# Conformer-and-RWKV-7 block on one core: TensorE's order in phase 1 written by the kernel instead of by the scheduler

## The chip, the cores and the metric

The kernel runs on one core of a Trainium2 chip. The core has TensorE (PE in the profile, with its weight loads as PEld), VectorE (DVE), ScalarE (ACT), GpSimd (POOL) and SyncE, whose queue (SPq) issues nearly all transfers. The metric is device time in microseconds (us) of one launch, lower is better. A difference under 0.5% (15 us here) can't be told from no change.

## The reference

```python
mod = silu(c) @ ada_w + ada_b                      # shift, scale, gate
h = rmsnorm(x, norm_g) * (1 + scale) + shift       # x: 2048 tokens x 1024
p = h @ w_in                                       # one projection for both branches
# branch A: u = val * sigmoid(gate); causal depthwise conv of width 31; layernorm; swish; * silu(c_og); @ w_conv_out
# branch B: token shift of r, k, v, w_low, a_low; decay and a from two low-rank products; then per token and head
state = state * w_t - (state @ kk_t) b_t^T + v_t k_t^T     # 16 heads, state 64 x 64
o_t   = state @ r_t
# layernorm of o per head, + sum(r*k*r_k)*v, * silu(r_og), @ w_rwkv_out
m = sigmoid(g_conv) * y_conv + sigmoid(g_rwkv) * y_rwkv
out = rmsnorm(x + gate * (m @ w_out), final_g)
```

All of it is float32.

## The kernel before

The 2048 tokens are taken in four blocks of 512 (`TB`), the channels in tiles of 128. A float32 projection is done as three products of a rounded high part and a low part (`hi*hi`, `lo*hi`, `hi*lo`, line 210, `mm3k`): eight steps of 128 input channels, three products each, and each product cut into two of 256 columns, so that one projection tile is 48 matmuls on line 217. Weights come as float32 in block 0, are split by ScalarE (line 194) and GpSimd or VectorE (line 196), and are written back to memory; later blocks read the two halves. Seven buffers hold them.

**Phase 1** goes through the four blocks. A block begins with eight loads of the normed input and their split into `h_hi` and `h_lo` (`hprep`, line 376) and the low-rank tile (`lora_split`). Then come four groups of four heads, two pairs of heads each. For a group these small products are needed beside its projections:

- `pair` (line 476), once for each of the two pairs: the low-rank products (489 to 495), then from k the sums of squares (528), from r and k the products inside chunks of 64 tokens (558, two batches), from v its transposes (581) and the head sums (297, 298), and the transposes of the keys (599, two batches). They go through three accumulator buffers, `aux`.
- the first products with v (628), whose result is copied into `XO`;
- the inverse of the triangular 64 x 64 matrices: eight small tiles of 16 KB a pair are sent to memory, laid out anew, solved by GpSimd in 31 steps of two operations (656, 658), sent back, transposed by VectorE (684), and two batches of 32 x 32 products on TensorE merge them (688, 697);
- the **chain** over the eight chunks: c1 (715, state times k and r) -> VectorE adds (717) -> c2 (720, inverse times that) -> VectorE scales into `uv` (722) -> c3 (726, keys times uv) -> VectorE updates the state `S` (730) -> next chunk. These are 24 TensorE steps a group, each waiting for VectorE, and each chain waits for the one before;
- the outputs (739), added on VectorE into the even half of `XO` (744), normed there by VectorE, ScalarE and GpSimd (756 to 765), transposed on TensorE (770) and written out. `XO` has one buffer, so the next group's `XO` is set to zero (617) after that.

The other projections (convolution values and gates, output gates) need nothing of this: they fill. Each convolution tile costs VectorE 31 operations over 512 columns (802, 805). `xnorm` (341) norms the next block's tokens and transposes them on TensorE (359). In block 3 its place is taken by the first layer norm (`lnorm_first`) and the first gated outputs (`z_first`). Side work that prepares the weights of phase 2 (`keep`, `ogate`) stands in blocks 1 and 2. **Phase 2** does the three output projections and the final norm.

What sets the order: the program is written group by group, and a list scheduler with a simulated timeline (`schedule_with_timeline_sim=True`) chooses, on each engine, the next instruction by what it believes ready and by program order, raised by `high_priority`. On the chip each engine then takes its instructions in that fixed order, and an instruction that waits holds up all behind it.

## Time and profile before

| what | us |
|---|---|
| median of 3 runs (2982.64 to 2993.91) | 2986.47 |
| the profiled execution, its span | 2988.9 |
| phase 1, to the last product with h | about 2390 |
| phase 2 | about 599 |
| TensorE busy in the span | 2817.8 |
| VectorE, ScalarE, GpSimd busy | 2053.9, 941.8, 1251.6 |

The profiled execution's own time is its span, 2.4 us over the median. In a row of groups the columns are line, engine, operation, result<-operands, shape, count, busy us, mean ns of one, idle us before it and what ended that. A row of waits has who waited, for whom, us in all, times, longest. A row of stages has length, then busy time and count for each engine, then the granted TensorE clock as a share. A float32 product of TensorE appears in the trace as two instructions, in the order below as one.

### The profile page before, as it was taken

The numbers are of one execution on the slowest core, as the hardware profiler recorded it, in microseconds if no ns is written. First come the engines' busy times: TensorE is split into PE (matmuls) and PEld (weight loads), VectorE is DVE, ScalarE is ACT, GpSimd is POOL, SyncE is SP. The second block draws the span as 40 slices with busy tenths as digits, with TensorE's granted clock in tenths as the row PEclk, the third lists the DMA queues.
The fourth block names the chain that finished last, engine by engine and source line by source line (L and its number), as shares of the span: only waits on it lengthen the run. The fifth ranks groups of instructions, "written<-read, shape, count | busy, mean of one in ns | idle before, by whom it ended". The sixth has DMA issues, their size and how long they took to land.

```text
span 2988.9 us, 64784 instructions
## 1 busy us (share of the span) xinstructions
PE 2817.8 (94%) x25672; PEld 2647.3 (89%) x25672; DVE 2053.9 (69%) x3871; ACT 941.8 (32%) x1779; POOL 1251.6 (42%) x1786
## 2 busy tenths in 40 slices
PE   6889898999999999899999999999999999899998
PEld 6889898989899998899989988999989978688988
DVE  6677878787677676867776667777689535777433
ACT  5433434342324142324132414132333112333201
POOL 3556455534343435243434445526367104555000
PEclk9999999999999999999999999999999999999999
DMA  8666758664758589647565767656547678889774
GB/s 313 216 229 217 254 212 281 239 225 158 259 189 288 158 267 300 220 150 245 160 229 169 254 227 260 200 181 204 175 159 263 219 273 304 326 300 341 243 284 167
DMA packets 367697, 699.24 MB, mean 234 GB/s; under 512 B 135265, under 2 KB 154017, under 8 KB 367394
## 3 DMA queue, kind: packets, MB, share of 16 engines
q1 hardware_dynamic: 367394, 695.10, 68.5%
q8 instruction: 202, 3.31, 0.4%
q14 instruction: 101, 0.83, 0.1%
HBM read 506.14 MB, written 187.70 MB: 232 GB/s over the span
## 4 chain that ended last, share of the span: by engine, by line
PE 42%; DMA 16%; POOL 10%; DVE 10%; SPq 4%; issue 4%; ACT 2%; POOLq 0%; DVEq 0%; ACTq 0%
PE ps_main L217 31%; POOL TT L658 4%; POOL itmp L656 3%; DMA La<-dA 2%; DMA w_st<-w_in_t 2%; DVE acc L805 2%; PE pout L1126 1%; PE pout L1127 1%; PE pout L1128 1%; DMA w_gr<-grow_d 1%; DMA dT<-TT 1%; DMA xt<-x_in 1%; DMA w_st<-w_ro_t 1%; SPq L669 1%; PE xo L720 1%
## 5 line engine op out<-in xcount | busy, mean ns | idle before, releaser
L217 PE MATMUL ps_main<-h_hi,w_lo 128*128 128x256 f32 x4608 | 952.4, 285 | 18.2 <-POOL w_lo L196 9.8
L217 PE MATMUL ps_main<-h_hi,w_hi 128*128 128x256 f32 x4608 | 952.0, 285 | 17.0 <-ACT w_hi L194 6.0
L217 PE MATMUL ps_main<-h_lo,w_hi 128*128 128x256 f32 x4608 | 951.1, 285 | 0.0
L217 PEld LDWEIGHTS ps_main<-h_hi,w_hi 128*128 128x128 f32 x4608 | 720.4, 192 | 28.7 <-ACT w_hi L194 10.5
L217 PEld LDWEIGHTS ps_main<-h_hi,w_lo 128*128 128x128 f32 x4608 | 719.1, 192 | 28.1 <-POOL w_lo L196 11.5
L217 PEld LDWEIGHTS ps_main<-h_lo,w_hi 128*128 128x128 f32 x4608 | 719.0, 191 | 7.2 <-issue 0.5
L805 DVE SCALAR_TENSOR_TENSOR acc<-u,ck,acc 128x512 f32<-128x512 f32 x928 | 697.4, 752 | 19.9
L656 POOL TENSOR_TENSOR itmp<-La,TT 128x126 f32<-128x126 f32 (+22 forms) x496 | 180.3, 363 | 161.5 <-DMA La<-dA 126.4
L658 POOL TENSOR_TENSOR TT<-TT,itmp 128x126 f32<-128x126 f32 (+22 forms) x496 | 190.2, 383 | 36.8
L712 ACT ACTIVATE Se<-S,pe 128x128 f32<-128x128 f32 x256 | 88.8, 394 | 252.6 <-DVE S L730 252.3
L196 POOL TENSOR_TENSOR w_lo<-w_st,w_hi 128x1024 fp32r<-128x1024 f32 x47 | 115.0, 2447 | 126.7 <-ACT w_hi L194 115.1
L730 DVE TENSOR_TENSOR S<-xo,Se 64x128 f32<-64x128 f32 x256 | 73.4, 287 | 104.0 <-PE xo L726 99.8
L194 ACT CAST w_hi<-w_st 128x1024 fp32r<-128x1024 f32 x71 | 74.5, 1049 | 177.8 <-DMA w_st<-w_in_t 137.0
L722 DVE TENSOR_TENSOR uv<-xo,rn 64x256 f32<-64x256 f32 x128 | 53.8, 420 | 97.1 <-PE xo L720 95.7
L593 POOL TENSOR_TENSOR BK<-BK,pe 128x1024 f32<-128x1024 f32 x32 | 62.3, 1946 | 111.2 <-PE aux L558 83.5
L717 DVE TENSOR_TENSOR XO<-xo,XO 128x256 f32<-128x256 f32 x128 | 53.6, 418 | 78.4 <-PE xo L715 63.5
L715 PE MATMUL xo<-S,KR 128*128 128x128 f32 x512 | 82.7, 284 | 18.6 <-DVE S L730 18.5
L568 DVE TENSOR_TENSOR As<-aux,maskA 128x512 f32<-128x512 f32 x128 | 82.9, 684 | 21.0 <-PE aux L558 20.2
L817 ACT ACTIVATE th<-ps_main 128x512 f32<-128x512 f32 x64 | 38.2, 597 | 187.2 <-PE ps_main L217 175.3
L720 PE MATMUL xo<-XO,As 64*64 64x64 f32 x1024 | 90.2, 227 | 6.2 <-DVE XO L717 6.2
L720 PEld LDWEIGHTS xo<-XO,As 64*64 64x64 f32 x1024 | 70.7, 135 | 26.9 <-DVE XO L717 8.1
L558 PE MATMUL aux<-KR,BK 64*128 64x128 f32 x1024 | 91.7, 295 | 2.1 <-POOL KR L546 1.7
(303 smaller groups left out, 5292.6 us busy)
## 6 DMA issues: line engine op xcount, KB each, us to landing
w_hi<-kh_in SPq DMA_DIRECT2D x219, 512.0 KB, 5.3
w_lo<-kl_in SPq DMA_DIRECT2D x219, 512.0 KB, 4.1
w_st<-w_in_t SPq DMA_DIRECT2D x73, 512.0 KB, 4.7
kh_in<-w_hi SPq DMA_DIRECT2D x71, 512.0 KB, 2.9
kl_in<-w_lo SPq DMA_DIRECT2D x71, 512.0 KB, 3.6
w_hi<-kh_ro SPq DMA_DIRECT2D x32, 512.0 KB, 6.3
w_lo<-kl_ro SPq DMA_DIRECT2D x32, 512.0 KB, 5.5
w_hi<-kh_co SPq DMA_DIRECT2D x32, 512.0 KB, 4.7
```

Of the source, the lines that this page charges most:

```text
L194: nc.scalar.copy(hi, st)
L196: lo_eng.tensor_tensor(out=lo, in0=st, in1=hi.bitcast(F32), op=ALU.subtract)
L217: nc.tensor.matmul(ps[:, qs], ww[:, k, :], aa[k][:, qs], start=(k == 0 and t == 0 and q == 0), stop=(k == KT - 1 and t == 2 and q == ms - ...
L558: return nc.tensor.matmul(pA[hh][:, c // 2, es], BK[hs, cc, es], KR[hs, cc, es], start=(c == 0), stop=(c == 3), skip_group_check=True)
L568: nc.vector.tensor_tensor(out=Asb[:, hh, c4 * 4:c4 * 4 + 4, :].rearrange("p (a e) n -> p a (e n)", e=2), in0=pA[hh], in1=flat(maskA).unsqu ...
L656: nc.gpsimd.tensor_tensor(out=tmp[:, :ni, :nt], in0=La[:, j:j + 1, j + 1:].broadcast_to([P, ni, nt]), in1=TT[:, :ni, j:j + 1].broadcast_to ...
L658: nc.gpsimd.tensor_tensor(out=TT[:, :ni, j + 1:], in0=TT[:, :ni, j + 1:], in1=tmp[:, :ni, :nt], op=ALU.add)
L712: nc.scalar.mul(Se[:, q, :], Sg[:, q, :], R[q]["pe"][:, c:c + 1])
L715: nc.tensor.matmul(xo[:, q, :], R[q]["KR"][:, cc, es], Sg[:, q, :], start=(q == 0), stop=(q == 1), skip_group_check=True)
L720: nc.tensor.matmul(xo[pr_, q, hs], As[q][pr_, hh, c, kcol(e)], XO[pr_, c, q, hs], start=(q == 0 and hh == 0), stop=(q == 1 and hh == 1), s ...
L730: nc.vector.tensor_tensor(out=Sg[hs, :, hs], in0=xo[hs, 2:4, hs], in1=Se[hs, :, hs], op=ALU.add)
L805: nc.vector.scalar_tensor_tensor(out=acc if i + 1 < HALO else yj, in0=u[:, i:i + TB], scalar=ck[:, j, i:i + 1], in1=acc, op0=ALU.mult, op1 ...
```

## The change

TensorE's order in phase 1 is no longer chosen by the scheduler (`manual_schedule` for that engine alone; the other engines and the queues are ordered as before). The small products are written as generators, *threads*, that hand back a condition and a least gap in us. `compose` runs a clock that only adds the planned length of every product issued (`te`). It issues the first thread, by rank, whose condition holds and whose gap is over; else one step (six matmuls) of the next projection; and if there is none it moves the clock by 0.25.

```diff
+LSQ, LKR, LA2, LVV, LTK, LUV = 6.0, 6.0, 2.4, 4.0, 2.4, 1.5
+LCH, LINV, LNORM, LXN, LLOW = 3.0, 68.0, 30.0, 20.0, 8.0
+LOOK, DUO, LSIDE = 10, 2, 12.0
+    def te(us):
+        clock[0] += us
+        return nc.tensor
+    def compose(jobs):
+        while jobs or threads:
+            t_ = next((t_ for t_ in sorted(threads, key=lambda t_: t_.rank) if t_.ready()), None)
+            if t_ is not None:
+                t_.resume()
+                continue
+            j_ = pick(jobs)
+            if j_ is None:
+                clock[0] += 0.25
+                continue
...
+            if next(j_[1], None) is None:
+                jobs.remove(j_)
...
+            if c:
+                yield lch
             xo = px.tile([P, 4, P], F32, name="xo", tag="xo")
             for q in range(2):
-                nc.tensor.matmul(xo[:, q, :], R[q]["KR"][:, cc, es], Sg[:, q, :], start=(q == 0), stop=(q == 1),
-                                 skip_group_check=True)
+                te(0.22).matmul(xo[:, q, :], R[q]["KR"][:, cc, es], Sg[:, q, :], start=(q == 0), stop=(q == 1),
+                   skip_group_check=True)
             nc.vector.tensor_tensor(out=XO[:, c], in0=xo[:, 0:2], in1=XO[:, c], op=ALU.add)
+            yield lch
...
-        O = XO[:, 0::2]
+        done.add(("chain", G))
+        O = uv[:, 0:NCH // 2]
...
+        yield last(G, LNORM, 22.0)
         for q in range(2):
             pr = 2 * g + q
+            yield (late_free, 0.0)
...
+    def merge(G):
+        yield (lambda: G in inv, 0.0)
+        As, rn, uv, R = grp[G]
+        T11, at = inv.pop(G)
+        yield (lambda: clock[0] >= at + last(G, LINV, 60.0) and late_free(), 0.0)
```

In words, what else it does:

- Gaps: three us (`LCH`) after each chain step, 68 (`LINV`; 60 in the last group) from the second pair's products inside chunks to the merges, 30 (`LNORM`) from the outputs to their transposes, 20 (`LXN`) in `xnorm`, 6, 4 and 2.4 between steps of a pair (`LSQ`, `LKR`, `LVV`, `LTK`).
- The inverse is issued in the second pair's thread, right behind its products inside chunks, and no longer after the whole pair and the first products with v.
- The outputs go into the first half of `uv` (two buffers) instead of `XO`, and are normed there.
- The priorities of the work on the other engines: chain, merge and norm of outputs 8000 (`HPC`), `xnorm` 6000 (`HPX`), pairs 4000 (`HPP`). The tanh of gates and the low-rank split get 3000, as the weights' splits have.
- Loads of `xnorm`, `hprep`, `keep`, `ogate`, `z_first` and others get a dependency without a semaphore on the last TensorE instruction issued (`behind`), which places them in the scheduler's order. `keep` and `ogate` are a thread with 12 us between the halves.
- Two projections at a block's end and two at its beginning are interleaved step by step (`duo`), so that the inputs `h` are used up, and taken up, tile by tile.
- In block 3 the filling projections are spread over the groups in another way (`LP`).
- The number of operations on each engine is unchanged but for five instead of six weight splits a group on VectorE in block 0.

**Where chain and products inside chunks meet.** TensorE before, in the second group of block 1. L726 is c3, L715 the next chunk's c1, L558 the products inside chunks of a later pair, L217 a projection; S_422 is the second group's state.

```order
L726 MATMUL xo<-uv,tk 128x128 x2
L217 MATMUL ps_main<-h_lo,w_hi 128x256 x2
L217 MATMUL ps_main<-h_hi,w_lo 128x256 x2
L558 MATMUL aux<-KR,BK 128x128 x9
L217 MATMUL ps_main<-h_hi,w_hi 128x256 x2
L217 MATMUL ps_main<-h_lo,w_hi 128x256
L715 MATMUL xo<-S_422,KR 128x128 x2
```

The same meeting now, in the group after it (S_424); c3 is L843, c1 L830, the products inside chunks L652, a projection L303.

```order
L843 MATMUL xo<-uv,tk 128x128 x2
L652 MATMUL aux<-KR,BK 128x128 x8
L303 MATMUL ps_main<-h_hi,w_hi 128x256 x2
L303 MATMUL ps_main<-h_lo,w_hi 128x256 x2
L303 MATMUL ps_main<-h_hi,w_lo 128x256 x2
L303 MATMUL ps_main<-h_hi,w_hi 128x256 x2
L303 MATMUL ps_main<-h_lo,w_hi 128x256 x2
L303 MATMUL ps_main<-h_hi,w_lo 128x256 x2
L303 MATMUL ps_main<-h_hi,w_hi 128x256 x2
L303 MATMUL ps_main<-h_lo,w_hi 128x256 x2
L303 MATMUL ps_main<-h_hi,w_lo 128x256 x2
L830 MATMUL xo<-S_424,KR 128x128 x2
```

Between the two chain steps stood 7 projection matmuls, and now stand 18. Counted over all 383 distances between neighbouring chain steps, those with fewer than 12 projection matmuls between went from 64 to 7, those with 12 to 23 from 128 to 65, those with 24 to 29 from 146 to 99, and those with 30 to 36 from 27 to 197.

**Small products of a pair.** TensorE before, in block 1: v's transposes (L581) and, later, the head sums (L297, L298).

```order
L581 MATMUL aux<-ident,vv 128x128 x4
L217 MATMUL ps_main<-h_hi,w_hi 128x256 x2
L217 MATMUL ps_main<-h_lo,w_hi 128x256 x2
L217 MATMUL ps_main<-h_hi,w_lo 128x256 x2
L217 MATMUL ps_main<-h_hi,w_hi 128x256 x2
L217 MATMUL ps_main<-h_lo,w_hi 128x256 x2
L217 MATMUL ps_main<-h_hi,w_lo 128x256 x2
L715 MATMUL xo<-S_420,KR 128x128 x2
L217 MATMUL ps_main<-h_hi,w_hi 128x256 x2
L297 MATMUL aux<-rh,bones 128x512
L298 MATMUL aux<-s_lo,bones 128x512
```

Now, in block 1 too: c2 (L836), v's transposes (L679), the head sums (L683, L684) and the other pair's low-rank products (L576 to L582) follow each other.

```order
L836 MATMUL xo<-XO,As 64x64 x4
L679 MATMUL aux<-ident,vv 128x128 x4
L683 MATMUL aux<-rh,bones 128x512
L684 MATMUL aux<-s_lo,bones 128x512
L576 MATMUL aux<-lw,wl 128x512
L577 MATMUL aux<-lw,wlo 128x512
L581 MATMUL aux<-la,wl 128x512
L582 MATMUL aux<-la,wlo 128x512
L449 MATMUL late<-ident,xt 128x128 x4
```

Such a meeting of low-rank products with v's products, with no projection between, stands at 8 places now, and stood at none.

**Where phase 1 ends.** TensorE before: the last product with h is the L217 row with h_hi and w_lo, the first of phase 2 the one with o_hi; the chain is that of the last group (S_426).

```order
L726 MATMUL xo<-uv,tk 128x128 x2
L217 MATMUL ps_main<-h_hi,w_lo 128x256 x2
L715 MATMUL xo<-S_426,KR 128x128 x2
L720 MATMUL xo<-XO,As 64x64 x4
L726 MATMUL xo<-uv,tk 128x128 x2
L715 MATMUL xo<-S_426,KR 128x128 x2
L217 MATMUL ps_main<-o_hi_30970,w_hi 128x512 x2
```

Now, with the output transposes of the group before (L892) among the chain steps:

```order
L303 MATMUL ps_main<-h_hi,w_lo 128x256 x2
L830 MATMUL xo<-S_426,KR 128x128 x2
L836 MATMUL xo<-XO,As 64x64 x4
L892 MATMUL late<-ident,uv 128x128 x4
L843 MATMUL xo<-uv,tk 128x128 x2
L892 MATMUL late<-ident,uv 128x128 x4
L830 MATMUL xo<-S_426,KR 128x128 x2
L836 MATMUL xo<-XO,As 64x64 x4
L303 MATMUL ps_main<-o_hi_30973,w_hi 128x512 x2
```

Four chain steps stood there with no projection between, now five do.

518 lines of the change are left out of this document (347 added, 171 removed).

## The prediction

> **What bounds it now.** I read the page first, for the engine that leaves no room.
>
> ```profile
> span 2988.9 us, 64784 instructions
> PE 2817.8 (94%) x25672; PEld 2647.3 (89%) x25672; DVE 2053.9 (69%) x3871; ACT 941.8 (32%) x1779; POOL 1251.6 (42%) x1786
> ```
>
> TensorE is busy 94% of the span; the next engine, VectorE, 69%. So the change can win only what TensorE loses in phase 1. How much that is, the stages tell: the columns are length, TensorE busy, its weight loads, VectorE, ScalarE, GpSimd, granted clock, transfers.
>
> ```profile
> 110.00:600.00 490.00, 460.83 (x4518) 441.65 (x4518) 369.23 (x620) 180.31 (x299) 268.13 (x379) 0.97 0.69 238
> 600.00:1200.00 600.00, 572.76 (x5777) 548.18 (x5776) 430.42 (x829) 193.17 (x374) 246.74 (x411) 0.99 0.70 230
> 1200.00:1870.00 670.00, 632.38 (x6356) 605.64 (x6356) 479.95 (x923) 213.37 (x410) 283.58 (x439) 0.98 0.65 213
> 1870.00:2190.00 320.00, 320.00 (x3268) 306.21 (x3268) 224.71 (x419) 89.88 (x168) 149.49 (x254) 1.00 0.58 189
> 2190.00:2390.00 200.00, 191.47 (x1916) 183.04 (x1916) 161.65 (x282) 56.27 (x96) 96.23 (x144) 0.97 0.67 218
> 2390.00:2989.00 599.00, 563.78 (x3282) 491.19 (x3280) 308.95 (x642) 147.78 (x316) 163.71 (x116) 0.97 0.77 279
> ```
>
> From 110 to 2390 us TensorE idles 29.2 + 27.2 + 37.6 + 0 + 8.5 = 102.6 us. It also runs below full clock: 0.03 x 490 + 0.01 x 600 + 0.02 x 670 + 0.03 x 200 = 40.1 us (the shares are rounded, so give or take 10). Together 142.7 us. The stage 1870 to 2190 is a check: no idle time, clock 1.00, and 320.00 / 3268 = 97.9 ns an instruction. The other four hold 18,567 instructions in 1960 us; at 97.9 ns they would take 1818, 142 less. So phase 1 without waits would be some 142 us shorter, with this kernel's own mix of products. The last stage is phase 2, which the change doesn't reorder.
>
> Who ends TensorE's idle time (waiter, released by: total, times, longest):
>
> ```profile
> PE xo L715 <- DVE S L730: 18.5, 16, 3.1
> ...
> PE late L770 <- POOL XO L765: 12.5, 8, 3.3
> PE xo L726 <- DVE uv L722: 12.0, 11, 3.1
> ...
> PE ps_main L217 <- POOL w_lo L196: 9.8, 7, 1.8
> PE ps_main L217 <- DMA w_lo<-kl_in: 8.3, 3, 6.1
> ...
> PE aux L599 <- POOL BK L593: 6.9, 6, 2.8
> PE aux L581 <- DVE vv L455: 6.5, 4, 2.6
> PE late L359 <- DVE xt L356: 6.4, 2, 4.9
> PE xo L720 <- DVE XO L717: 6.2, 9, 1.0
> PE late L688 <- DVE T L684: 6.0, 2, 5.5
> PE ps_main L217 <- ACT w_hi L194: 6.0, 2, 3.8
> PE ps_main L217 <- DVE carry L457: 4.6, 3, 3.6
> ```
>
> There is no one culprit: small products that were placed too near to what they need, many times, for one to three us each. One such place in the second group of block 1, on TensorE and then on VectorE:
>
> ```profile
> 977.32 0.39 PE L217 MATMUL ps_main<-h_hi,w_hi 128*128 128x256 f32 x2
> 977.55 0.39 PE L217 MATMUL ps_main<-h_lo,w_hi 128*128 128x256 f32 x2
> ...
> 979.31 0.71 PE L726 MATMUL xo<-uv,tk 128*128 128x128 f32 x4 [0.24 <-DVE uv L722]
> 979.77 0.49 PE L217 MATMUL ps_main<-h_lo,w_hi 128*128 128x256 f32 x2
> 980.10 0.39 PE L217 MATMUL ps_main<-h_hi,w_lo 128*128 128x256 f32 x2
> ...
> 983.98 0.68 PE L715 MATMUL xo<-S,KR 128*128 128x128 f32 x4 [1.64 <-DVE S L730]
> ```
>
> ```profile
> 981.34 1.99 DVE L356 TENSOR_SCALAR xt<-xt,ss 128x512 f32<-128x512 f32 x2
> 983.26 0.58 DVE L730 TENSOR_TENSOR S<-xo,Se 64x128 f32<-64x128 f32 x2
> ```
>
> c3 is done at 980.0; VectorE takes the state's update up only at 983.3, behind two operations of `xnorm`; c1 stands seven projection matmuls and a batch of products after c3, and TensorE stands still for 1.64 us. The clock pays too (granted clock 0.54 in the next 3.6 us):
>
> ```profile
> 984.60:988.20 3.60, 3.60 (x21) 3.38 (x21) 1.92 (x5) 0.71 (x2) 0.00 (x0) 0.54 0.65 220
> ```
>
> **The change, part by part**, against the span of 2988.9. All sizes below that no row gives outright are my estimates from the rows named.
>
> *Chain.* The three waits are 18.5 + 12.0 + 6.2 = 36.7 us. 192 of 383 distances were under 24 projection matmuls, now 72. If waits went with them, 72/192 of 36.7 = 14 would stay. The chain also ranks above `xnorm` and the pairs on VectorE now, which is what went wrong at 983. I take -30; bounds 0 and -36.7.
>
> *Output transposes*, 12.5: they move behind 30 us of planned products. The longest wait was 3.3 us, and a distance that grows by about five covers it (estimate: some 211 matmuls stood there, 24 us at the 0.23 per two of 977.32 to 977.55). -12; bounds 0 and -12.5.
>
> *Steps of a pair* (keys 6.9, v 6.5): gaps of 2.4 and 4 us against longest waits of 2.8 and 2.6: -9 of 13.4. *`xnorm`*, 6.4: nearly all of it one wait of 4.9, at the start, now with 20 us: -4.
>
> These are -55. *Clock:* 40.1 / 102.6 = 0.39 us of half rate for each idle one, so another -21. [...]
>
> *Projections' own waits* (weights 9.8 + 8.3 + 6.0, accumulator 4.6: 28.7): no gap bears on them. Gates' tanh gets priority, `xnorm`'s loads no longer bunch ahead of weights, `duo` stretches the change of block. A quarter: -7, and -3 of clock; bounds 0 and -28.7. `behind` puts no semaphore on the queue, so it costs the chip nothing.
>
> *Breaks* in the projection stream: 639 runs in the whole order, now 588. A projection behind a small product took 0.33 per two instead of 0.23 (979.77 to 980.10 beside 977.32 to 977.55): 51 x 0.1 = -5.
>
> *Costs.* Eight places put low-rank products straight behind v's products; the fourth accumulator they need is one of three, and comes back only after two copies of
>
> ```profile
> L583 ACT COPY uv<-aux 64x512 f32<-64x512 f32 x64 | 37.1, 580 | 62.4 <-PE aux L581 62.0
> ```
>
> 1.16 us. Part of it lies under the products between: 8 x 1 = +8; bounds 0 and +16. At the end of phase 1 one more chain step and two transposes stand uncovered:
>
> ```profile
> 2391.26 0.68 PE L715 MATMUL xo<-S,KR 128*128 128x128 f32 x4 [0.61 <-DVE S L730]
> 2392.46 0.68 PE L720 MATMUL xo<-XO,As 64*64 64x64 f32 x8 [0.52 <-DVE XO L717]
> ```
>
> An uncovered step takes 1.2 us: +2 with the transposes.
>
> *Inverse.* From the last product inside chunks (L558) to the last of VectorE's transposes (L684), first in the tenth group, then in the last:
>
> ```profile
> 1432.73 0.27 PE L558 MATMUL aux<-KR,BK 64*128 64x128 f32 x1
> 1488.74 0.29 DVE L684 STREAM_TRANSPOSE T<-As 32x128 f32<-32x128 f32 x1
> 2252.76 1.16 PE L558 MATMUL aux<-KR,BK 64*128 64x128 f32 x14
> 2334.32 0.29 DVE L684 STREAM_TRANSPOSE T<-As 32x128 f32<-32x128 f32 x1
> ```
>
> 56 and 81 us. The merge stood well behind that; now it stands 68 planned us after (60 in the last group), the plan counts no waits, and all of TensorE's queue is behind it. Most groups will fit and a few won't: +10; bounds 0 and what the last rival below gives. The inverse is issued earlier now, which helps.
>
> *At nothing:* the outputs in `uv`. The operations are the same and lie beside projections; `XO` comes free sooner, so a chain no longer waits for the norm before it. `uv` is held longer, but has two buffers. If GpSimd's norm came late, the transposes' wait would come back, 12.5.
>
> Sum: -55 - 21 - 10 - 5 + 8 + 2 + 10 = -71. 2988.9 - 71 = 2917.9 for a profiled execution; the runs' median lay 2.4 under that, so 2915.5.
>
> **Rivals.**
>
> *A clean phase 1.* Gaps, priorities and steady loads take away all 102.6 + 40.1, and the breaks 5: 2841, median 2839. For it speaks the stage 1870 to 2190, which had no wait under the old order. Against it: that stage has no `xnorm` and no side work, and the weights of block 0.
>
> *The clock doesn't follow.* Half-rate stretches are not owed to the short waits, and stay: -55 - 7 - 5 + 20 = -47, 2942, median 2939.5. [...] The row at 984.6 speaks against it.
>
> *The waits move.* VectorE, ScalarE and GpSimd are ordered by the same scheduler, with the same wrong ideas of when things come. If the wait only goes from c1 to whatever the gaps put in the place of it, only the breaks' 5 remain: 2984, median 2981.5. For it: the waits are many and spread. Against it: the distances did grow.
>
> *The merge holds up TensorE (slower).* If the inverse took 81 us in every group, the merge would wait 81 - 68 = 13 us in 15 groups and 21 in the last: 216 us. Each wait is followed by some 3.4 us at half rate, as at 984.6, 1.7 lost: 16 x 1.7 = 27. Against that stand -81 of the other terms: +162, so 3151, median 3148.5. It decides from 81 / 16 - 1.7 = 3.4 us a group: an inverse of 71.4 us on average eats the whole gain, one of 72.3 makes the kernel slower by over 15 us. Between 56 and 81 that is not far. Against it: it now starts earlier, and its GpSimd steps rank with the pairs.
>
> **How the numbers follow.** Forecast 0.51, clean phase 1 0.15, no clock 0.10, waits that move 0.12, merge 0.12. A measurement of this kernel tells 0.5%, 15 us, from no change. Forecast, clean and no clock are faster by more: 0.76. Waits that move: within, 0.12. Merge: slower, 0.12. The forecast alone reaches from 2875 to 2945: the bounds of its terms add up to about -141 and +13, and don't all fall on one side. The range, 2848 to 2990, adds no clock, waits that move and half of the clean case, and leaves out the merge and the other half, 0.19.
>
> **What would show it.** Right: TensorE's waits on S, uv and XO fall from 36.7 to under 10; those on the normed outputs vanish; clock 0.99 or more in the stages of phase 1; phase 1 ends 65 to 80 us earlier; phase 2 keeps its 599. Wrong: a wait of L778 (the merge) on the transposed tile of 3 us or more in most groups; new waits on `aux` tiles where low-rank and v's products meet, over 16 us in all; the clock's share unchanged although the waits fell; waits on weights above 28.7.

## The result, and the profile after

The changed kernel is a little slower: 3002.17 us median against 2985.59, a ratio of 1.0053 with a 95% interval of 1.0039 to 1.0067. The forecast, 2915.5 us with a range up to 2990, was wrong in sign. The loss itself is small, about the 0.5% from which a change can be told at all; the miss, 86 us beside the forecast, is not. The profiled execution after has a span of 3004.0 us, 15.1 more than before.

First the page after: span, and the engines' busy time (share of the span, instructions).

```profile
span 3004.0 us, 64670 instructions
...
PE 2797.4 (93%) x25672; PEld 2635.1 (88%) x25672; DVE 2007.5 (67%) x3867; ACT 940.5 (31%) x1779; POOL 1262.7 (42%) x1790
```

TensorE's idle time is the span less its busy time: 171.1 us before, 206.6 after, +35.5. Its busy time is 20.4 less. The two make the 15.1. So the change did two things that nearly cancel: the same 25672 products took less time, and TensorE stood still for longer. The clock doesn't explain the shorter time of the products: its mean was 0.977 before and is 0.971, which by itself would add some 0.029 x 3004.0 - 0.023 x 2988.9 = 18 us (an estimate), part of it in idle time. At an equal clock, then, the products take 20 to 38 us less.

The stages after, in the same columns as in the prediction:

```profile
110.00:600.00 490.00, 453.05 (x4416) 435.04 (x4415) 356.07 (x631) 182.94 (x304) 275.12 (x361) 0.96 0.68 229
600.00:1200.00 600.00, 565.78 (x5752) 543.93 (x5751) 426.75 (x837) 192.78 (x375) 256.51 (x438) 0.97 0.70 231
1200.00:1870.00 670.00, 633.93 (x6470) 609.79 (x6468) 479.91 (x937) 206.46 (x397) 271.86 (x435) 0.97 0.65 213
1870.00:2190.00 320.00, 293.56 (x2925) 280.65 (x2923) 217.40 (x395) 100.62 (x179) 172.32 (x244) 0.96 0.60 202
2190.00:2403.00 213.00, 206.25 (x2205) 198.91 (x2205) 151.29 (x289) 50.16 (x95) 79.30 (x159) 0.99 0.56 185
2403.00:3004.00 601.00, 563.70 (x3300) 489.03 (x3300) 307.20 (x644) 149.95 (x320) 171.44 (x116) 0.98 0.78 279
```

Phase 1 ends at 2403 and not at 2390, and phase 2 keeps its length. The stage 1870 to 2190, which had no idle time before, now has 26.4 us. What ends TensorE's waits after (waiter, released by: total, times, longest):

```profile
PE late L449 <- DVE xt L443: 17.8, 3, 10.5
...
PE ps_main L303 <- DMA w_lo<-kl_in: 15.3, 5, 6.1
PE xo L836 <- DVE XO L832: 13.0, 11, 3.5
PE xo L830 <- DVE S L847: 10.1, 9, 2.4
PE ps_main L303 <- DVE th L921: 9.8, 4, 3.8
...
PE ps_main L303 <- ACT th L960: 8.2, 1, 8.2
PE ps_main L303 <- DMA w_hi<-kh_in: 8.0, 1, 8.0
...
PE late L892 <- POOL uv L885: 6.9, 1, 6.9
...
PE aux L581 <- ACT uv L681: 5.5, 6, 3.7
PE ps_main L303 <- POOL w_lo L282: 5.2, 4, 1.7
...
PE ps_main L303 <- ACT w_hi L280: 4.3, 3, 1.7
PE xo L843 <- DVE uv L838: 4.2, 3, 1.6
PE late L892 <- ACT oc L895: 4.1, 2, 3.8
...
PE aux L679 <- DVE vv L540: 3.7, 3, 2.4
```

The chain's three waits fell from 36.7 to 13.0 + 10.1 + 4.2 = 27.3. `xnorm`'s rose from 6.4 to 17.8. Waits on weights rose from 24.1 to 15.3 + 8.0 + 5.2 + 4.3 = 32.8. Waits on accumulators that VectorE and ScalarE had not yet emptied (`th`) rose from 2.0 to 9.8 + 8.2 = 18.0. The projections with h, one row for each of the three products, and the products inside chunks, of the kernel before and then of the changed one (busy us, mean ns | idle time in front of them; instructions of different rows overlap, so that the rows add up to more than the busy time of the page):

```profile
L217 PE MATMUL ps_main<-h_hi,w_lo 128*128 128x256 f32 x4608 | 952.4, 285 | 18.2 <-POOL w_lo L196 9.8 <-DMA w_lo<-kl_in 8.3
L217 PE MATMUL ps_main<-h_hi,w_hi 128*128 128x256 f32 x4608 | 952.0, 285 | 17.0 <-ACT w_hi L194 6.0 <-DVE carry L457 4.6 <-DVE acc L805 2.1
L217 PE MATMUL ps_main<-h_lo,w_hi 128*128 128x256 f32 x4608 | 951.1, 285 | 0.0
L558 PE MATMUL aux<-KR,BK 64*128 64x128 f32 x1024 | 91.7, 295 | 2.1 <-POOL KR L546 1.7 <-DVE As L568 0.2
```

```profile
L303 PE MATMUL ps_main<-h_hi,w_hi 128*128 128x256 f32 x4608 | 972.7, 293 | 42.5 <-DVE th L921 9.8 <-ACT th L960 8.2 <-DMA w_hi<-kh_in 8.0
L303 PE MATMUL ps_main<-h_lo,w_hi 128*128 128x256 f32 x4608 | 917.7, 281 | 0.7 <-DVE h_lo L463 0.7
L303 PE MATMUL ps_main<-h_hi,w_lo 128*128 128x256 f32 x4608 | 917.4, 281 | 21.0 <-DMA w_lo<-kl_in 15.3 <-POOL w_lo L282 5.2 <-DVE w_lo L282 0.5
...
L652 PE MATMUL aux<-KR,BK 64*128 64x128 f32 x1024 | 80.8, 293 | 9.3 <-DVE As L655 4.9 <-POOL TT L725 2.4 <-POOL KR L638 1.9
```

Idle time in front of projections went from 35.2 to 64.2 us: +29.0, most of the 35.5. Their busy time went from 2855.5 to 2807.8, that of products inside chunks from 91.7 to 80.8.

The longest wait for `w_lo`, on SyncE's queue and then on TensorE:

```profile
1060.96 1.34 SPq L736 DMA_DIRECT2D dT<-TT  x2
...
1065.65 11.59 SPq L743 DMA_DIRECT2D As<-dT  x16
...
1078.28 0.40 SPq L274 DMA_DIRECT2D w_lo<-kl_in  x1
```

```profile
1076.14 0.39 PE L303 MATMUL ps_main<-h_lo,w_hi 128*128 128x256 f32 x2
1082.66 0.58 PE L303 MATMUL ps_main<-h_hi,w_lo 128*128 128x256 f32 x1 [6.13 <-DMA w_lo<-kl_in]
```

The inverse's 16 small stores hold SyncE for 11.6 us (the longest of the 16 such blocks in this trace, which take 7.7 to 11.6); the next `w_lo` is issued at 1078.3, and TensorE, out of weights at 1076.5, stands for 6.13 us. The longest wait of `xnorm` but one, on VectorE (first and last operation of its short chain) and on TensorE:

```profile
978.71 0.16 DVE L439 TENSOR_TENSOR ss<-ss 128x1 f32<-128x1 f32 x1 [0.38 <-ACT xsq L436]
978.79 0.75 DVE L943 SCALAR_TENSOR_TENSOR acc<-u,ck,acc 128x512 f32<-128x512 f32 x1
...
997.27 1.30 DVE L443 TENSOR_SCALAR xt<-xt,ss 128x512 f32<-128x512 f32 x2
```

```profile
998.23 1.11 PE L449 MATMUL late<-ident,xt 128*128 128x128 f32 x4 [7.00 <-DVE xt L443]
```

Operations of 0.15 us alternate with taps of 0.75 us and with work of the chain and the pairs: from the first operation to the start of the last it takes 18.6 us on VectorE alone, after the loads and the squares, and the gap of 20 had to hold all of it.

### The profile page after: what moved, and what is told of

It is laid out like the page before. It is cut to its first block, busy times and chain, and to the rows that moved or that the text cites. A ratio compares the mean times of both kernels' runs of the same rounds, so it can differ in the third digit from the quotient of the medians.

```text
span 3004.0 us, 64670 instructions
## 1 busy us (share of the span) xinstructions
PE 2797.4 (93%) x25672; PEld 2635.1 (88%) x25672; DVE 2007.5 (67%) x3867; ACT 940.5 (31%) x1779; POOL 1262.7 (42%) x1790
## 4 chain that ended last, share of the span: by engine, by line
PE 51%; DVE 16%; DMA 14%; POOL 9%; issue 4%; SPq 3%; ACT 3%; DVEq 0%; POOLq 0%; ACTq 0%
PE ps_main L303 36%; DVE acc L943 5%; DMA w_st<-w_in_t 4%; POOL TT L732 3%; POOL itmp L730 3%; POOL w_lo L282 2%; PE pout L1355 2%; PE xo L836 2%; PE pout L1357 2%; PE pout L1356 2%; PE aux L652 1%; SPq L743 1%; PE xo L830 1%; DMA La<-dA 1%; DMA w_hi<-kh_in 1%
## 5 line engine op out<-in xcount | busy, mean ns | idle before, releaser
L303 PE MATMUL ps_main<-h_hi,w_hi 128*128 128x256 f32 x4608 | 972.7, 293 | 42.5 <-DVE th L921 9.8
L303 PE MATMUL ps_main<-h_hi,w_lo 128*128 128x256 f32 x4608 | 917.4, 281 | 21.0 <-DMA w_lo<-kl_in 15.3
L303 PE MATMUL ps_main<-h_lo,w_hi 128*128 128x256 f32 x4608 | 917.7, 281 | 0.7 <-DVE h_lo L463 0.7
L303 PEld LDWEIGHTS ps_main<-h_hi,w_hi 128*128 128x128 f32 x4608 | 714.2, 192 | 67.3 <-issue 14.1
L303 PEld LDWEIGHTS ps_main<-h_hi,w_lo 128*128 128x128 f32 x4608 | 710.4, 191 | 23.3 <-DMA w_lo<-kl_in 16.5
L303 PEld LDWEIGHTS ps_main<-h_lo,w_hi 128*128 128x128 f32 x4608 | 713.5, 192 | 1.3 <-DVE h_lo L463 1.3
L282 POOL TENSOR_TENSOR w_lo<-w_st,w_hi 128x1024 fp32r<-128x1024 f32 x51 | 123.3, 2417 | 123.8 <-ACT w_hi L280 115.7
L620 POOL TENSOR_TENSOR ta<-ta,k 128x512 f32<-128x512 f32 x32 | 46.3, 1448 | 158.4 <-ACT ta L619 158.4
L536 ACT ACTIVATE t<-ps_main,mu 128x512 f32<-128x512 f32 x96 | 65.7, 684 | 144.8 <-PE ps_main L303 132.5
L836 PE MATMUL xo<-XO,As 64*64 64x64 f32 x1024 | 87.1, 226 | 13.0 <-DVE XO L832 13.0
L836 PEld LDWEIGHTS xo<-XO,As 64*64 64x64 f32 x1024 | 69.5, 135 | 32.1 <-DVE XO L832 14.6
L686 POOL TENSOR_TENSOR vv<-rk,vv 128x512 f32<-128x512 f32 x32 | 41.7, 1302 | 115.2 <-ACT rk L685 109.6
```

Source lines behind the costliest of these rows:

```text
L282: lo_eng.tensor_tensor(out=lo, in0=st, in1=hi.bitcast(F32), op=ALU.subtract)
L303: lastpe[0] = te(0.113 * 2 / ms).matmul(ps[:, qs], ww[:, k, :], aa[k][:, qs], start=(k == 0 and t == 0 and q == 0), stop=(k == KT - 1 and ...
L536: nc.scalar.activation(t1, ps, AF.Identity, scale=mu1[:, mi:mi + 1])
L836: te(0.155).matmul(xo[pr_, q, hs], As[q][pr_, hh, c, kcol(e)], XO[pr_, c, q, hs], start=(q == 0 and hh == 0), stop=(q == 1 and hh == 1), s ...
```

## The experiments

Ratios are against the kernel before, with 95% intervals; the changed kernel stands at 1.0053. A line of waits or of time from a run comes from its one profiled execution. The expectations speak of four theories. Theory 1: the fixed order does its own part, and what the plan's clock does not count (weights behind unbroken blocks of stores in SyncE's queue; evictions, which are the reads that empty an accumulator; `xnorm`'s chain) came up as waits, while the kernel before was spared since the scheduler's simulation counts those things. Theory 2: the gaps are too short. Theory 3: the new priorities push other work back. Theory 4: the outputs in `uv` cost.

**e1: the outputs in `uv` alone.**

The edit, in the kernel before:

```diff
-        O = XO[:, 0::2]
+        O = uv[:, 0:NCH // 2]
```

> The kernel before with one part of the change alone: the normed outputs are computed in uv and not in XO; TensorE's order stays with the scheduler. Theory 1 (the fixed order does its own part, and what its clock does not count, weights behind SyncE's small stores, evictions and xnorm's chain, came up as new waits): 0 us, within 6 us either way, since the 12.5 us of waits on normed outputs are not for a buffer. Theory 4 (outputs in uv hold uv, two buffers, longer, and the next groups wait for it): 8 to 16 us slower, the whole of the change's loss.

Measured: 0.9986 (0.997 to 1.0001). Theory 4 falls. The part of the change that was costed at nothing costs nothing that can be measured.

**e2: the order given back.**

The region in which TensorE keeps the order of the program text is gone:

```diff
-    ctx_pe = tc.manual_schedule(engines={mybir.EngineType.PE})
...
-    ctx_pe.__enter__()
...
-    ctx_pe.__exit__(None, None, None)
```

> The changed kernel with TensorE's order given back to the scheduler: the same threads, priorities and places in the program text, but no fixed order on TensorE. Theory 1: the scheduler's simulation counts weights, evictions and SyncE's queue again, so projections' own waits come back from 67 us to 36 to 45, and the chain's waits rise; 2975 to 3000 us, at or a little below the changed kernel. Theory 3 (the new priorities 8000, 6000 and 4000 push splits, evictions and loads back on the other engines, whoever orders TensorE): still 3000 us or more, with projections' own waits above 55 us.

Measured: 1.0117 (1.0094 to 1.0139), outside theory 1's range and slow enough for theory 3. But the waits are not as theory 3 has them: TensorE waits less in front of projections (4.1 + 0.6 us for transfers of weights, 1.8 for VectorE's `th`). From the page:

```profile
PE 2873.7 (95%) x25672; PEld 2691.6 (89%) x25672; DVE 2042.1 (68%) x3867; ACT 938.8 (31%) x1779; POOL 1257.7 (42%) x1790
```

Idle time is 3019.9 - 2873.7 = 146.2 us, 60 less than with the fixed order; busy time is 76.3 more at the same mean clock, 0.971. Counted in the traces, from the first to the last product with h, TensorE changes from one line's products to another's 1,612 times in the kernel before, 1,450 times in the changed one and 1,725 times here. So without a fixed order (and without the old pins, the `issue_after` of the kernel before, which the change took out) the scheduler waits little and breaks up more. The fixed order trades the other way: unbroken products for waits.

**e3: the inverse's stores from GpSimd's queue.**

```diff
-                        nc.sync.dma_start(As[q][sl, hh, e::2, sl], dT[:, q, hh, :, e, bk, :])
+                        nc.gpsimd.dma_start(As[q][sl, hh, e::2, sl], dT[:, q, hh, :, e, bk, :])
```

> The changed kernel with the 16 stores As<-dT of each inverse issued from GpSimd's queue and not from SyncE's, where they held back weight loads for 8 to 12 us at a time. Theory 1: the stalls of TensorE right behind those blocks (2.9, 6.1, 8.2, 3.2, 1.7, 4.3, 8.0, 3.1 us, 37 together, against 8 in the kernel before) go for the greater part: 20 to 35 us faster than the changed kernel, 2967 to 2982 us. Theory 2 (the gaps are too short everywhere, and weights only came up where TensorE would have waited anyway): within 6 us of the changed kernel.

Measured: 1.0135 (1.011 to 1.016), slower. Yet the waits on weights are gone, and others have taken their place:

```profile
PE late L778 <- DVE T L749: 18.9, 10, 4.4
PE ps_main L303 <- DVE th L921: 18.6, 6, 5.0
...
PE aux L652 <- POOL KR L638: 14.4, 3, 12.2
...
PE aux L652 <- POOL BK L622: 10.2, 1, 10.2
...
PE ps_main L303 <- DMA w_lo<-kl_in: 2.5, 1, 2.5
```

Weights: 2.5 here, 2.5 for GpSimd's `w_lo` and 1.6 for `w_hi`, 6.6 in place of 32.8. GpSimd, now held by the stores (at their line it stands idle 61.7 us until the writes of dT have landed, and 41.4 us under "issue"), is late with the operands of the products inside chunks, and the stores reach the merge later: its wait on the transposed tile went from 2.2 to 18.9 us. The first half of theory 1 stands (the blocks make weights late); as a cure the edit fails.

**e4: `xnorm`'s gap 36.**

```diff
-LCH, LINV, LNORM, LXN, LLOW = 3.0, 68.0, 30.0, 20.0, 8.0
+LCH, LINV, LNORM, LXN, LLOW = 3.0, 68.0, 30.0, 36.0, 8.0
```

> The changed kernel with the gap between xnorm's loads and its transposes at 36 us and not 20 (the chain of 13 small VectorE operations took about 30). Theory 1: the waits on xt of 10.5 and 7.0 us go and nothing takes their place: 12 to 18 us faster than the changed kernel, 2984 to 2990 us. Rival (the order only moves: what stands behind then waits for something else): within 6 us of the changed kernel.

Measured: 1.0017 (1.0003 to 1.003), some 11 us off the changed kernel, between the two ranges. The wait on `xt` is gone (TensorE waits 1.7 us there, for ScalarE). In the profiled execution, 6.7 us under this kernel's median, idle time only fell from 206.6 to 2984.2 - 2784.2 = 200.0, and the mean clock was 0.977 (0.975 in the median of its runs). So this gap was too short, and other waits took most of its place.

**e5: with that, the chain's gap 3.5.**

```diff
-LCH, LINV, LNORM, LXN, LLOW = 3.0, 68.0, 30.0, 36.0, 8.0
+LCH, LINV, LNORM, LXN, LLOW = 3.5, 68.0, 30.0, 36.0, 8.0
```

> The changed kernel with xnorm's gap at 36 us, as in the run before, and the chain's least gap at 3.5 us and not 3.0 (2.8 for the last group, as it was). Theory 2 (the gaps are too short): the chain's waits of 29 us in that run (c1 11.5, c2 11.2, c3 6.6) fall below 10 and the time by 12 to 20 us, to a ratio of 0.995 to 0.998. Theory 1 (a wait goes to whichever engine's work is late, and VectorE is late by one tap of 0.75 us or by several, not by half a microsecond): the chain's waits fall by 5 to 12 us, projections' own 76 us stay; ratio 0.998 to 1.002.

Measured: 1.0107 (1.0092 to 1.0123), slower than either theory said. The chain's waits went from 30.2 to 12.3 + 7.9 + 6.7 = 26.9. The last product with h starts in the same place, at 2384.1 us beside 2383.2 in e4, but the chain's last product starts at 2517.0 us and not at 2470.6. From 2384 to the end, in e4 and in e5:

```profile
2384.00:2984.00 600.00, 564.46 (x3299) 489.75 (x3297) 308.39 (x644) 149.82 (x319) 167.50 (x116) 0.97 0.78 280
```

```profile
2384.00:3017.00 633.00, 577.34 (x3588) 500.60 (x3586) 323.87 (x678) 154.59 (x330) 173.40 (x120) 0.96 0.73 268
```

289 more instructions are left for the time after the last projection with h, and that time is 33 us longer, which is the whole loss. Each group has 23 gaps, a half us more in each makes 11.5 us, and over the groups the chain falls behind the projections and pays at the end.

**e6: the stores and loads of the inverse merged over the heads** (with e4's gap). The stores; the loads dA<-As are merged in the same way:

```diff
-                    for hh in range(2):
-                        nc.sync.dma_start(As[q][sl, hh, e::2, sl], dT[:, q, hh, :, e, bk, :])
+                    nc.sync.dma_start(As[q][sl, :, e::2, sl], dT[:, q, :, :, e, bk, :])
```

> The changed kernel with xnorm's gap at 36 us and the inverse's loads and stores of As merged over the two heads: 8 and 8 transfers in place of 16 and 16, of twice the bytes. Theory 1 (SyncE's unbroken blocks of small transfers hold back weight loads; with the stores on GpSimd the waits on weights fell from 33 to 7 us, but GpSimd then held up the pairs): if an issue costs the same whatever it moves, the blocks halve and the waits on weights fall from 42 us to under 25; 12 to 20 us faster than the run with the gap alone, ratio 0.995 to 0.998. If the issue's time goes with the bytes: no change, within 5 us. Theory 2: no change either way.

Measured: 0.9956 (0.9939 to 0.9973), faster than the kernel before. One block on SyncE's queue:

```profile
1186.47 5.52 SPq L741 DMA_DIRECT2D As<-dT  x8
```

This is one of the longer blocks here (the median of 16 is 4.5 us, beside 8.6 in the changed kernel). Over all stores of a trace one issue takes 0.45 us at 32 KB here, 0.46 us at 16 KB in the changed kernel and 0.45 us at 8 KB in e9: it went with the number of transfers and not with the bytes. Waits on weights went from 41.6 in e4 to 25.4 + 1.6 + 1.4 = 28.4, and 16.3 of that is one wait. That is 13 us less, of the 18 gained.

**e7: evictions and splits first** (with e4's gap).

```diff
-HP = 3000
+HP = 9000
```

> The changed kernel with xnorm's gap at 36 us and the priority of what follows a projection (weight splits, gates' tanh, the products with them) at 9000 and not 3000, ahead of the threads' 4000, 6000 and 8000. Theory 3 (the new priorities push evictions and splits back): the projections' own waits on evictions and casts (34 us) and on split weights (11 of the 42) halve, the chain's rise by under 5 us; ratio 0.994 to 0.998. Theory 1: those waits come from work that already stands in VectorE's and ScalarE's queues when the eviction comes due; within 6 us of the run with the gap alone, ratio 1.000 to 1.004.

Measured: 1.0014 (1.0 to 1.0029), the same as e4. Theory 3 falls, as far as the priority of evictions and splits goes.

**e8: the merged transfers in the kernel before.** The edit of e6.

> The kernel before with the inverse's loads and stores merged in the same way, as a control. Theory 1: the scheduler's simulation put TensorE's order around SyncE's queue already, and of its 24 us of waits on weights only some 8 stand behind such blocks; 0 to 8 us faster, ratio 0.997 to 1.000. If the merged transfers help both kernels alike (12 us or more here), the queue is no cause of what the change lost.

Measured: 1.0024 (1.001 to 1.0038), a shade slower and outside both ranges. The kernel before gains nothing from the edit that gained the changed one 18 us.

**e9: 32 stores of half the bytes** (with e4's gap).

```diff
-                        nc.sync.dma_start(As[q][sl, hh, e::2, sl], dT[:, q, hh, :, e, bk, :])
+                        for cp in range(2):
+                            nc.sync.dma_start(As[q][sl, hh, e + 4 * cp:e + 4 * cp + 3:2, sl],
+                                              dT[:, q, hh, 2 * cp:2 * cp + 2, e, bk, :])
```

> The changed kernel with xnorm's gap at 36 us and the inverse's stores As<-dT in 32 transfers of half the bytes in place of 16 (the loads stay 16): the dose of SyncE's unbroken blocks doubled, where the run with merged transfers halved it and gained 17 us. Theory 1: an issue costs 0.56 us at 16 KB and 0.69 us at 32 KB, so it goes with the number; blocks of 9 us become 16 to 18 us, and the waits on weights and on what comes behind a late store rise: 15 to 35 us slower than the run with the gap alone, ratio 1.007 to 1.013. If the gain of the merged run came from the fewer loads dA<-As, or from the order that was dealt anew: within 6 us, ratio 1.000 to 1.004.

Measured: 1.0386 (1.0362 to 1.0411): the direction of theory 1, three times its size. TensorE's longest groups of waits:

```profile
PE ps_main L303 <- DMA w_lo<-kl_in: 73.8, 11, 20.4
PE ps_main L303 <- DMA w_hi<-kh_in: 31.2, 2, 25.6
```

With 12.0 for `w_hi` and 6.5 for `w_lo` this is 123.5 us on weights; 28.4, 41.6 and 123.5 for 8, 16 and 32 stores. The median block here takes 16.7 us. It is no straight line; one reading is that a block costs little as long as the weights loaded ahead cover it, and from there its whole excess (argued from the three doses, not shown block by block).

**e10: the chain's gap 3.5 in the first 12 groups alone** (on e6).

```diff
-        lch = last(G, LCH, 2.8)
+        lch = 3.5 if G < 12 else last(G, LCH, 2.8)
```

> The kernel of the merged transfers with the chain's gap at 3.5 us in the first 12 groups alone and as it was (3.0, 2.8) in the last four; with 3.5 in nearly all of them the last group's chain fell behind the last product with h, and phase 2 took 30 us more. Theory 2 (the gaps are too short, and only the end was spoilt): the chain's waits of 32 us fall by 12 to 18, ratio 0.990 to 0.993. Theory 1 (the chain waits for VectorE work that is late by more than half a microsecond): by 3 to 8 us, ratio 0.993 to 0.996.

Measured: 0.9931 (0.9906 to 0.9956), the fastest kernel here that does all the work, 2969.54 us beside 2986.93. The chain's waits fell by 7 (33.3 in e6; 12.2 + 9.8 + 4.3 = 26.3 here), inside theory 1's 3 to 8; those on weights fell as well, from 28.4 to 16.7 with the same eight stores, so that the order too has a say in them. Its time lies where the two theories' ranges meet, and the interval overlaps e6's: it beats both kernels of the change, but that it beats e6 is not shown.

**e11: dT written from GpSimd's queue** (on e6).

```diff
-            nc.sync.dma_start(dTl[half], TT[64 * half:64 * half + 64])
+            for qr in range(2):
+                nc.gpsimd.dma_start(dTl[half][32 * qr:32 * qr + 32], TT[64 * half + 32 * qr:64 * half + 32 * qr + 32])
```

> The kernel of the merged transfers with the inverse's result TT written to dT from GpSimd's queue, in four pieces, and not from SyncE's in two: SyncE waited 34 us for TT there, and 26 us more under other lines behind it, with weight loads queued behind. Theory 1: the waits on weights (29 us) fall below 18, GpSimd pays 2 us for each of 16 groups where nothing waits for it; 6 to 14 us faster than the merged run, ratio 0.991 to 0.994. Rival (GpSimd is as tight as SyncE, as with the 16 stores there): 0 to 10 us slower.

Measured: 1.0124 (1.0104 to 1.0143), 50 us worse than e6. What GpSimd's idle time ended on:

```profile
POOL dT L736 <- issue: 129.2, 42, 6.0
```

That is 8 us of idle time for each inverse, and SyncE then waits 124.0 us for dT (21.5 in e6). The rival was right, and by more than it said.

**e12: the inverse's transposes on VectorE late** (on e6): they move from the inverse to 6 us ahead of the merge, tied behind TensorE's last product there.

> The kernel of the merged transfers with VectorE's transposes of the inverse, which stood in its queue waiting 41 us for the stores As<-dT with conv taps and evictions behind them, issued 6 us of the plan's clock ahead of the merge and not at once. Theory 1, second half (evictions come late because VectorE's queue is held by that wait): the waits on evictions and casts (28 us) fall by 8 to 12 and VectorE's wait on the stores below 8; 6 to 14 us faster than the merged run, ratio 0.991 to 0.994. Rival (VectorE has time to make up for it; the evictions come late for other reasons): within 5 us.

Measured: 0.9963 (0.9936 to 0.9989), the same as e6. VectorE's wait on the stores fell from 41.1 to 8.0 us as meant. TensorE's wait on `th` was 15.1 us, not less than e6's 10.8. So VectorE's wait for the stores is not what makes evictions late.

**e13 and e14: no stores As<-dT at all,** in the kernel before and in the changed one. Both leave out work that the result needs.

```diff
-        nc.vector.tensor_scalar(out=rq, in0=pss, scalar1=L2_EPS * L2_EPS, scalar2=-1.0, op0=ALU.max, op1=ALU.mult)
+        nc.vector.tensor_scalar(out=rq, in0=pss, scalar1=L2_EPS * L2_EPS, scalar2=-1.0e4, op0=ALU.max, op1=ALU.mult)
...
-                        nc.sync.dma_start(As[q][sl, hh, e::2, sl], dT[:, q, hh, :, e, bk, :])
```

> The kernel before without the inverse's 16 stores As<-dT (left out; the normalising factor is scaled by 1e-4, so that the values stay finite), for the share of SyncE's small stores in the time of the kernel before. Theory 1 (the scheduler ordered TensorE around them): 0 to 12 us faster, ratio 0.996 to 1.000. Rival (the stores cost both kernels alike, and the change's loss lies elsewhere): as much as in the changed kernel without them, 20 us or more, ratio below 0.994.

> The changed kernel without the inverse's 16 stores As<-dT (left out, with the same scaling). Theory 1: waits on weights fall from 33 us to under 12, what stands behind late h loads and late transposes goes as well; 25 to 45 us faster than the changed kernel, ratio 0.990 to 0.997 against the kernel before, so below the same kernel before without stores. Rival: the gain is the same as in the kernel before, within 8 us.

Measured: 0.9899 (0.9872 to 0.9927) for the kernel before, 0.9800 (0.9774 to 0.9826) for the changed one. The stores cost the kernel before 1.0%, the changed one 2.5%: 30 and 75 us. Both gains are larger than theory 1 gave, nor are they alike, as the rival would have it: the stores cost both kernels, and the changed one 45 us more. Without them the new order is the faster by 28 us, less than half of the forecast 71. The runs also take away the wait of the transposes and of the merge for the stores, so the two costs are those of the stores with all that hangs on them, not of SyncE's blocks alone. Waits of TensorE in e14:

```profile
PE ps_main L303 <- DVE th L914: 5.2, 3, 2.0
...
PE ps_main L303 <- DMA w_lo<-kl_in: 3.0, 2, 2.0
```

What is left on weights is 3.0 + 3.6 + 1.6 + 1.0 us. The waits on `th` nearly halved too (18.0 to 5.2 + 4.8 = 10.0). Idle time is 2925.8 - 2769.0 = 156.8, the clock 0.981.

**e15: 32 stores in the kernel before.** The edit of e9.

> The kernel before with 32 stores of half the bytes in place of 16, as in the changed kernel where it cost 110 us. Theory 1: the scheduler's simulation sees the longer blocks and puts other products ahead, so far less: 10 to 40 us, ratio 1.003 to 1.013. Rival (the scheduler knows no more of the queue than the fixed order does): 70 to 120 us, ratio 1.023 to 1.040.

Measured: 1.0513 (1.0488 to 1.0538), 150 us, more than in the changed kernel. That is the rival's side and beyond it, and the second half of theory 1 falls in this form: the old order is not proof against these blocks. But it is another wait that grew:

```profile
PE late L689 <- DVE T L685: 72.4, 37, 7.9
PE late L698 <- DVE Qs L693: 27.2, 13, 3.4
```

Waits on weights stay at 5.7 + 5.4 + 3.8 + 2.9 = 17.8 us, beside 123.5 in e9. In 14 of the 16 groups TensorE starts the merge 1 to 22 us before the inverse's last tile is transposed; in e9, where the plan puts the merge 68 us of products behind the pair's last product inside chunks, in 4. So the one order is hit at the merge, the other at its weights; whether TensorE's stand at the merge is what gives the weights time to arrive, no run shows.

**e16: 11 taps of 31** in the changed kernel.

```diff
-            for i in range(HALO):
+            for i in range(20, HALO):
```

> The changed kernel with 11 of the convolution's 31 taps (20 left out): VectorE, whose queue the chain's sums, the evictions and xnorm's chain share with the taps of 0.75 us, has 480 us less to do of some 1700 in phase 1. If its queue is what makes them late: the waits on the chain (26 us), on evictions by VectorE (15), on xnorm (18) and on products inside chunks (9) fall by two thirds, 35 to 50 us faster than the changed kernel, ratio 0.988 to 0.994, with the 33 us on weights left. If they are late for other reasons (the order, the length of each small chain): under 15 us faster, ratio 1.000 to 1.005.

Measured: 0.9895 (0.9869 to 0.9921), 1.6% off the changed kernel, inside the range for a full queue on VectorE (the kernel leaves out 20 taps, so this is no gain that can be had). In its parts the expectation fails: the chain's waits only fell from 27.3 to 7.4 + 5.5 + 4.9 = 17.8, those on VectorE's `th` from 9.8 to 7.2; `xnorm`'s from 17.8 to 4.6 + 1.7 and the normed outputs' from 12.0 to 1.6. Waits on weights, forecast to stay at 33, fell to 15.6 + 1.9 + 1.6 + 1.0 = 20.1. VectorE's load made long chains of small operations late (`xnorm`'s wait); of the chain's waits it made up a third (9.5 of 27.3 us), not two thirds.

**e17 and e18: the 8 stores from ScalarE's queue, all of them, and half of them** (on e10).

```diff
-                    nc.sync.dma_start(As[q][sl, :, e::2, sl], dT[:, q, :, :, e, bk, :])
+                    nc.scalar.dma_start(As[q][sl, :, e::2, sl], dT[:, q, :, :, e, bk, :])
```

and for e18

```diff
-                    nc.sync.dma_start(As[q][sl, :, e::2, sl], dT[:, q, :, :, e, bk, :])
+                    (nc.scalar if bk else nc.sync).dma_start(As[q][sl, :, e::2, sl], dT[:, q, :, :, e, bk, :])
```

> The fastest kernel so far (xnorm's gap 36 us, 8 merged stores, chain's gap 3.5 us in the first 12 groups) with the 8 stores issued from ScalarE's queue. The changed kernel without any stores was 77 us faster than with its 16 on SyncE. Theory 1 (only the place in SyncE's in-order queue costs): ScalarE, idle for half of the time, pays 8 times 0.7 us for each group, and most of what 8 stores still cost comes back: 15 to 35 us faster, ratio 0.981 to 0.988. Rival (whichever engine issues them is held for as long, as GpSimd was, and tanh, casts and copies out of the accumulators come late): 0 to 30 us slower, ratio 0.993 to 1.003.

> The same with 4 of the 8 stores issued from ScalarE's queue and 4 from SyncE's. Theory 1: the block on SyncE is 2.8 us and the one on ScalarE as long, and neither outlasts the slack of its consumers: 10 to 25 us faster than the fastest so far, ratio 0.985 to 0.990. Rival (ScalarE, held, makes evictions late): within 8 us of it, ratio 0.991 to 0.996.

Measured: 0.9978 (0.9964 to 0.9992) and 0.9936 (0.9916 to 0.9957), beside e10's 0.9931. Both rivals hold. In e17 the waits on weights in phase 1 fell from e10's 16.7 to 3.6 + 1.6 + 1.4 = 6.6 (with 0.5 for VectorE's `w_lo`; 3.8 more are put down to a cast of weights for phase 2, L260, that these products don't read), and those on accumulators to be emptied (`th`) rose from 7.6 + 3.0 + 2.6 = 13.2 to 14.1 + 10.7 + 10.4 = 35.2:

```profile
PE ps_main L303 <- DVE th L919: 14.1, 6, 4.1
...
PE ps_main L303 <- ACT th L958: 10.4, 5, 3.0
```

Three queues, one finding: whoever issued the stores was held, by the wait for dT ahead of them and by the issues (SyncE for 7.7 to 11.6 us a block in the changed kernel, GpSimd for 61.7 + 41.4 us in e3, ScalarE for 23.2 us ahead of two gates' tanh in e17), and what waited behind on that engine became TensorE's wait. On weights TensorE waited less (32.8 us down to 6.6 in e3, 16.7 down to 6.6 in e17), but ScalarE and GpSimd paid that time out of their own work (waits on `th` 13.2 up to 35.2 us in e17, 14.4 + 10.2 us on operands of the products inside chunks in e3).

The stores in numbers (ratio to the kernel before with its 16):

| stores for each inverse | kernel before | changed kernel |
|---|---|---|
| 0 (e13, e14) | 0.9899 | 0.9800 |
| 8, loads merged too (e8, e6 with the gap 36) | 1.0024 | 0.9956 |
| 16 (e4 with the gap 36) | 1 | 1.0053 (1.0017) |
| 32 (e15, e9 with the gap 36) | 1.0513 | 1.0386 |

The new order is ahead by 0.7 to 1.3% at 0, 8 and 32 stores and behind at 16 alone, by 0.5%, or 0.2% with the gap 36. Each edit of the kernel before also makes the scheduler deal its order anew, which may be why its column doesn't rise evenly with the number of stores (not tested). So the 16 stores as they stand met the old order well; why they did, no run settles.

## Why the prediction was wrong, point by point

*The chain, -30; output transposes, -12; steps of a pair, -9; `xnorm`, -4.* The steps that failed are "a distance that grows by about five covers it" and 72/192 of the chain's waits left. Measured: chain 36.7 to 27.3 (-9.4), output transposes 12.5 to 6.9 + 4.1 + 1.0 = 12.0 (-0.5), keys and v 13.4 to 3.7 (-9.7, right), `xnorm` 6.4 to 17.8 (+11.4): -8 in place of -55, 47 of the 86 us between the forecast -71 and the measured +15. Places that had hardly waited now do: products inside chunks 2.1 to 9.3, low-rank products 5.5 on copies. The gap is counted in planned products, and the wait depends on when another engine gets to a small operation. e4 shows it for `xnorm` (20 was too short for a chain that alternates with taps), e5 and e10 for the chain: a gap half a microsecond longer took 3 to 7 us of about 30, and e16 that with a third of the taps two thirds of the chain's waits are still there.

*Projections' own waits, -7.* The step "no gap bears on them" failed, and with it the quarter taken off for loads that "no longer bunch ahead of weights": +29 (64.2 in place of 35.2) and not -7, a miss of 36, the largest of any wait taken by itself. Gaps move them (in e10 half a microsecond in the chain's gap went with 12 us less of waits on weights), and above all what stands in SyncE's queue does. The prediction did not look at the stores of the inverse, although each of them is an issue on the same queue. e3, e14 and e17 took the stores off SyncE, e18 half of them, and the waits on weights were between 6.6 and 10 us each time; e9 doubled the stores and the waits tripled. e13 and e14 give a size: with all that hangs on them, 16 stores cost the changed kernel 45 us more than the kernel before. Not all of the +29 is weights: those rose by 8.7, the waits on `th` by 16.

*Clock, -21.* It was tied to the idle time, and idle time rose: the mean clock went from 0.977 to 0.971, some +18 us. As a rule of thumb it held in sign (e14: 156.8 us idle, 0.981; e9: 285.7, 0.955), but not as a ratio: e2 had the least idle time of all, 146.2 us, and 0.971. In the traces of the two kernels half clock came behind every stretch of 3.41 us at full clock in which TensorE was busy for less than 43%, 18 and 24 of them (last section); the idle time in all does not show how it is spread over such stretches. The rival in which half clock is not owed to the short waits is not borne out: in the kernel before, 18 of the 26 falls to half clock came where TensorE stood idle for at most 3.27 us at a time.

*Breaks, -5.* Right in its direction, the size four to eight times too small: products took 20 to 38 us less at an equal clock, and e2 shows 76 us of busy time between the fixed order and the same program without it. What was missed is that products inside chunks and other batches were broken up too, not only the projection stream: 162 changes between products fell away (1,612 to 1,450), of which the projection stream, 610 runs before and 555 after, makes some 110. That they are the cause of the shorter time fits both pairs of kernels, and was not tested by itself.

*Meeting of low-rank and v's products, +8:* 5.5 us of waits on copies, right. *End of phase 1, +2:* phase 2 took 601 and 599 us, right. *Inverse late, +10, and the rival that the merge holds up TensorE:* waits at L778 on the transposed tile were 2.2 us in all; the rival did not come. From the last product inside chunks to the last transposed tile it took 55 to 83 us, 66.1 on average; the plan counts no waits, so that the merge stood not 68 but 79 us on average behind that product and covered all but two of the sixteen. *At nothing, `uv`:* right by e1, although the transposes' wait stayed for GpSimd's norm, as the text said it might.

Of the rivals, *the waits move* was the right one in kind, with a chance of 0.12. Even it had no mechanism by which they would grow, so its 2981.5 was still too low. "Waits on weights above 28.7" was named as a sign of failure, and came: 32.8 (the 28.7 hold 4.6 for an accumulator, and weights alone were 24.1).

Not settled: why the waits on emptied accumulators rose. Priorities (e7) and late transposes (e12) are not it; without the stores (e14) nearly half of them go, which points to something behind the same blocks, and the rest has no shown cause.

## What to carry to other kernels

An order fixed by hand can pack the engine better and lose as much again in waits for what its plan does not count (here 20.4 us less busy time against 35.5 us more idle time), so cost both. Before fixing it, list for each thing the engine reads which in-order queue brings it, and the longest unbroken block in that queue beside the time that what is loaded ahead covers. Shorten such a block (fewer, larger transfers: 8 of 32 KB in place of 16 of 16 KB took the median block from 8.6 to 4.5 us, and the kernel, with the loads merged too, from 1.0017 to 0.9956) before moving it: on GpSimd's queue (e3, 1.0135) and on ScalarE's (e17, 0.9978 beside e10's 0.9931) it held up that engine's work instead.

## What the runs showed of the hardware that was not expected

A small transfer into strided blocks of `As` cost its queue 0.45 us in the mean at 8 KB (e9), 0.46 at 16 KB (changed kernel) and 0.45 at 32 KB (e6); the median block took 16.7 us for 32 of them in e9, 8.6 for 16 in the changed kernel and 4.5 for 8 in e6, with the next weight loads behind it on SyncE. GpSimd issuing the four writes of dT in e11 was held for 8 us an inverse (129.2 us of "issue"). In e17 ScalarE stood behind the stores, and behind the wait for dT ahead of them, for 23.2 us ahead of two gates' tanh alone, 12.9 us of it in one place:

```profile
ACT th L918 <- DMA As<-dT: 23.2, 2, 12.9
```

In e2 TensorE ran at half its clock for 16.8 us although the longest wait in the 28 us before was 1.0 us. The waits of 1195 to 1224 us, and the granted clock (third column from the end) of the stretch behind them:

```profile
PE late L778 <- DVE T L749: 1.3, 2, 1.0
```

```profile
1223.40:1240.20 16.80, 12.90 (x139) 11.30 (x138) 14.81 (x30) 6.40 (x11) 0.00 (x0) 0.50 0.84 298
```

In that stretch itself TensorE was busy for 12.9 of 16.8 us. What brought the half clock on there, no run shows.

The clock records of the traces say more. In the kernel before, the granted clock in them is 1.0 or 0.5, and each record but the last is 3.41 us long or a multiple of that; half clock came for 3.41 to 10.24 us at a time. Cut into stretches of 3.41 us, the trace has 826 at full clock, and 26 of them are followed by half clock. TensorE was busy for less than 43% of the stretch in 18 of the 26, and in none of the 800 others; the remaining 8 lie between 50% and 79%, where 33 stretches of the others lie too. In the changed kernel it is 24 of 30, and none of 790. Of the 26, 18 touch no idle time of TensorE as long as 3.41 us, the longest in each being 0.74 to 3.27 us, and 4 of the 800 touch one of 3.5 to 6.9 us and kept their clock. These are counts of two traces; what decides between 43% and 79%, no run here shows. Half clock lasted 142 us in all before and 175 after, which agrees with the two means.
